# Moving the squares and root of a norm ahead of held-back matrix products in a hybrid encoder layer

## The chip, the cores and the metric

One core of one Trainium2 chip runs the whole layer. The metric is the device time of one execution in microseconds (us); the time before is the median of three executions. Besides these there is one profiled execution, on which every number of the trace rests. The engines are named as in the profile: PE is the matrix engine (PEld its weight loads), DVE the vector engine, ACT the scalar engine, POOL the general-purpose engine, SP the engine that issues most transfers.

## The reference

A layer has a mixer and a gated feed-forward network (FFN), each between two RMS norms:

```python
h = x + rmsnorm(mixer(rmsnorm(x, g_mix_pre)), g_mix_post)
y = h + rmsnorm(conv_ffn(rmsnorm(h, g_ffn_pre)), g_ffn_post)

def conv_ffn(h):
    gate, up = split(h @ w_up)                   # 1024 -> 2 x 2816
    gate_c = causal_dwconv(gate)                 # width 3
    return (gelu(gate_c) * up) @ w_down          # 2816 -> 1024
```

The mixer has one input projection, eight heads of stick-breaking attention, a state-space part with eight heads, and one output projection. There are 2048 prompt rows and 32 sample rows, 1024 features each, in float32. The root of a norm, `rsqrt(mean(h*h) + eps)`, is one number per row.

## The kernel before

Features lie on the partitions and rows (tokens) along the free axis. Every large product is made of three matmuls of rounded halves (hi by hi, hi by lo, lo by hi), recorded in `dense` (L124).

**Stages.** The rows are worked in four blocks `s` = 0 to 3 of 512, 512, 512 and 544 rows. After the input projection of all blocks and the attention of block 0, `build` runs a loop over the blocks: the tail of block `s` (output projection, residual, FFN) is a Python generator, `Tail.stream`, and is fed step by step as filler into the attention of block `s + 1`. A step is one group of three matmuls. For block 3 no attention is left, and its tail runs alone. In the texts "stage s" is the stretch in which the tail of block `s` runs.

**The tail of a stage** (`stream`): eight steps owed by the stage before; `out_units` for half a of the rows (0 to 256 or 272), eight units; `out_units` for half b, with the residual of half a advanced by one feature group every fourth step; the residual of half b; `split` for both halves; the rest of what is owed, 24 steps of the previous block's last down products, held back from its own stage; `root` for both halves; then 22 FFN units `up`, with `down` in groups, and `finish` of the previous block advanced at every second step from unit 1 on.

**What each of these does.** A unit of `out_units` leaves one of eight feature groups in `m[c]` (ACT copy, L915) and adds its square to `msq`. `residual` takes the post-norm's root from `msq`, then for each of the eight groups loads `x` into `xr` (two buffers), scales `m[c]` (DVE, L931), adds `x` (POOL and DVE in turn, L935) and stores it. `split` makes hi (ACT, L948) and lo (DVE, L949) of `m[c]` times the FFN gain. `root` squares and sums the eight `m[c]` again, now for the FFN's input norm, and takes the root with `rstd_narrow`. `up` multiplies the gate product by that root `r` as it leaves PSUM (L984), so the matmuls of `up` need `split` alone.

**Shared buffers.** `square` (L754) writes its square straight into the sum for the first group (L758); for the other seven ACT squares into `sqt` (L761), of which there is one buffer, and POOL adds (L762). All sums of squares use this one `sqt`: those of `out_units` (`msq`), of `root` (`msq` again), of the down products (`fsq`, L1058) and of the attention (`sq`). `rstd_steps` takes two tiles of the PSUM tile `u`, of which there is one buffer: for the column sums (L166), and for the root broadcast again over partitions (L195), which ACT copies out (L201). In stages 0 to 2 the second product of each FFN unit, `up`'s L1006 to L1013, is written to the same `u`; the gate products go to `o`, which has two buffers. In stage 3 the FFN products go to `t` and `o`.

**Order.** The program states an order; a list scheduler that works with simulated times then sets the order of each engine's queue when the kernel is built, and may put an instruction ahead of an earlier one that isn't ready. `pin` and `mark` keep the filler's matmuls behind the attention's matmuls issued ahead of them. On the chip each queue runs in its fixed order.

Of the kernel before, what the change touches and what calls it, by code (L numbers as in the profile page):

```python
# [57 lines left out]
def tiles_of(n):  # L58
    return [(0, n)] if n <= 512 else [(0, n // 2), (n // 2, n)]
# [810 lines left out]
class Tail:  # L870
# [48 lines left out]
    def residual(self, s, half):  # L919

        kn, nc, att = self.kn, self.kn.nc, self.att
        t0 = SBS[s][0]
        c0, c1 = half
        n = c1 - c0
        rm = att.tmp.tile([P, 272], F32, name="rstd")
        kn.rstd_narrow(att.tmp, *kn.bank, [self.msq[:, c0:c1]], n, D, out=rm)
        yield
        for c, m in enumerate(self.m):
            x = (self.late or att.tmp).tile([P, 272], F32, name="xr", bufs=8 if self.late else 2)
            nc.sync.dma_start(x[:, :n], kn.a["xT"][:, c, t0 + c0 : t0 + c1])  # L930
            nc.vector.scalar_tensor_tensor(  # L931
                m[:, c0:c1], m[:, c0:c1], kn.col(C_GMIXP + c), rm[:, :n], op0=ALU.mult, op1=ALU.mult
            )
            eng = nc.vector if c % 2 else nc.gpsimd
            eng.tensor_tensor(m[:, c0:c1], m[:, c0:c1], x[:, :n], op=ALU.add)  # L935
            nc.sync.dma_start(kn.hS[s][:, c, c0:c1], m[:, c0:c1])
            yield

    def split(self, s, half):
# [14 lines left out]
    def root(self, s, half):  # L954
        kn, nc, att = self.kn, self.kn.nc, self.att
        c0, c1 = half
        if c0 == 0:
            self.r = self.rp.tile([P, 544], F32, name="r", bufs=1)
        for c, m in enumerate(self.m):
            att.square(self.msq[:, c0:c1], m[:, c0:c1], c == 0)  # L960
        col = self.rp.tile([P, 8], F32, name=f"rcol{int(c0 > 0)}")
        kn.rstd_narrow(att.tmp, *kn.bank, [self.msq[:, c0:c1]], c1 - c0, D, out=self.r[:, c0:c1], rcol=col)
        self.cols[s, c0] = col
# [116 lines left out]
    def stream(self, s, cat):  # L1080
        nt = SBS[s][1]
        a, b = (0, nt // 2), (nt // 2, nt)
        owed, self.owed = self.owed or iter(()), None
        yield from islice(owed, 8)
        yield from self.out_units(s, cat, a)
        chain = self.residual(s, a)
        for n, _ in enumerate(self.out_units(s, cat, b)):
            yield
            if n % 4 == 0:
                next(chain, None)  # L1090
        for _ in self.residual(s, b):
            pass
        self.split(s, a)
        self.split(s, b)
        yield from owed
        self.root(s, a)
        self.root(s, b)
        done = iter(())
        if s:
            done = (i for h in (0, SBS[s - 1][1] // 2) for i in self.finish(s - 1, h, h + 256, self.f))  # L1100
        groups = self.GROUPS
        tiles = tiles_of(nt)
        acts = {}
        for g, (j0, n) in enumerate(groups):
            acts[g] = []
            for j in range(j0, j0 + n):
                for i, _ in enumerate(self.up(s, j, acts[g])):
                    yield
                    if j and i % 2:
                        next(done, None)  # L1110
                if j == j0 and g and g < len(groups) - 1:
                    yield from self.down(s, g - 1, acts.pop(g - 1), tiles)
        g = len(groups) - 1

        def last():
            for t in [tiles] if s < NSB - 1 else [[t] for t in tiles]:
                for e in range(2):
                    yield from self.down(s, g - 1 + e, acts[g - 1 + e], t, e == 1)
                if s == NSB - 1:
                    for _ in self.finish(s, *t[0], self.f):  # L1120
                        pass

        self.owed = last()
# [167 lines left out]
```

## Time and profile before

| | us |
|---|---|
| median of three executions | 3099.98 (3099.88 to 3104.38) |
| the profiled execution, its own time | 3103.09 |
| its span, first to last instruction | 3101.2 |
| PE busy in the span | 2883.8 |
| DVE, POOL, ACT busy | 1690.6, 1364.9, 1236.7 |
| POOL, sums of squares into `msq` (L762) | 112 instructions of 721 to 1707 ns |
| mean granted PE clock | 0.965 of full speed |

In rows of a timeline the columns are the start, the duration, the engine and line, the operation, its tiles (out<-in), how many instructions are merged, and in brackets the idle time before it with what ended it. In rows of stretches (windows) they are the stretch, its length, each engine's busy time with its count of instructions, the granted clock of PE, the share of DMA and GB/s. In rows of one line they are the count, the shortest, median and longest duration in ns, and when the first and the last began.

### The profile page before, as it was taken

Reading aid. Unit: us, or ns where it says so; the run is one execution under the profiler, and the core shown is the slowest. Engines: PE = TensorE matmul, PEld = TensorE weight load, DVE = VectorE, ACT = ScalarE, POOL = GpSimd, SP = SyncE. Lnnn points to the kernel's source line nnn. Section 1 sums busy time; section 2 is a strip of 40 time slices with the busy share of each in tenths; the row PEclk is TensorE's granted clock in tenths of the full one; section 3 lists DMA queues with packets and bytes.
Section 4 is the critical chain, followed back from the end, with each engine's and each line's share of the span. In section 5 each row is a group of like instructions: output and inputs, shape, how many; then the busy total and the mean of one; then the engine's idle time right before and its main releaser. Section 6 shows DMA issues by size and latency. Waiting matters only on the chain.

```text
span 3101.2 us, 43193 instructions
## 1 busy us (share of the span) xinstructions
PE 2883.8 (93%) x16175; PEld 2345.9 (76%) x16175; DVE 1690.6 (55%) x2388; ACT 1236.7 (40%) x2504; POOL 1364.9 (44%) x1073
## 2 busy tenths in 40 slices
PE   8999999987879999998899999988999999899996
PEld 6777778865747787785577788855777779799996
DVE  6667667656685643439844443398444324523334
ACT  4344444355565443346633322466433213321111
POOL 4555454355777665547732221376322214511113
PEclk9999999999889999998899999999999999899998
DMA  4545454565655778875264455742645554555455
GB/s 169 175 144 175 138 170 116 165 206 179 234 186 190 246 262 274 277 253 177 89 207 166 165 193 180 251 144 82 211 159 174 201 194 154 175 193 177 165 187 168
DMA packets 234658, 571.57 MB, mean 184 GB/s; under 512 B 49514, under 2 KB 101362, under 8 KB 205906
## 3 DMA queue, kind: packets, MB, share of 16 engines
q1 hardware_dynamic: 234450, 568.81, 55.3%
q8 instruction: 129, 2.11, 0.3%
q14 instruction: 79, 0.65, 0.1%
HBM read 435.22 MB, written 133.50 MB: 183 GB/s over the span
## 4 chain that ended last, share of the span: by engine, by line
PE 62%; DVE 17%; DMA 6%; POOL 6%; ACT 4%; issue 4%; SPq 1%; DVEq 0%; POOLq 0%; ACTq 0%
PE o L124 32%; PE u L124 10%; PE t L124 9%; DVE prow L659 4%; PE pa L837 3%; PE pt L822 2%; POOL beta L664 2%; PE z L801 2%; PE o L365 2%; DVE xc L341 1%; DVE acB L436 1%; POOL msq L762 1%; DMA acB<-acD 1%; DVE f L1072 1%; DVE xc L337 1%
## 5 line engine op out<-in xcount | busy, mean ns | idle before, releaser
L124 PE MATMUL o<-xhi,w 128*128 128x512 f32 (+2 forms) x3968 | 1037.5, 346 | 38.3 <-DMA w<-wS_out 8.8
L124 PEld LDWEIGHTS o<-xhi,w 128*128 128x128 f32 x3968 | 698.2, 192 | 138.8 <-issue 16.9
L124 PE MATMUL o<-xlo,w 128*128 128x512 f32 (+2 forms) x1984 | 684.9, 345 | 9.0 <-DVE xlo L273 4.2
L109 POOL TENSOR_TENSOR w<-wraw,w 128x1024 fp32r<-128x1024 f32 (+2 forms) x156 | 377.0, 2417 | 252.6 <-ACT w L108 237.9
L664 POOL TENSOR_TENSOR beta<-beta,prow 128x512 f32<-128x512 f32 (+3 forms) x264 | 313.5, 1192 | 335.0 <-DVE prow L659 317.5
L124 PEld LDWEIGHTS o<-xlo,w 128*128 128x128 f32 x1984 | 381.0, 192 | 55.5 <-DVE xlo L273 6.0
L1005 POOL TENSOR_TENSOR y<-y,gb 128x512 f32<-128x512 f32 (+1 forms) x88 | 118.3, 1344 | 597.9 <-ACT gb L1004 589.1
L659 DVE TENSOR_TENSOR_SCAN prow<-gam,prow 128x513 f32<-128x513 f32 x200 | 321.0, 1610 | 82.8 <-ACT gam L656 75.2
L124 PE MATMUL u<-xhi,w 128*128 128x512 f32 x1056 | 347.6, 400 | 2.2 <-DVE y L1014 2.1
L124 PE MATMUL o<-ah,w 128*128 128x512 f32 x992 | 334.5, 403 | 9.0 <-DVE f L1051 8.8
L124 PEld LDWEIGHTS u<-xhi,w 128*128 128x128 f32 x1056 | 200.4, 190 | 54.6 <-issue 4.2
L822 PE MATMUL pt<-ident,beta 128*128 128x128 f32 x1088 | 186.4, 293 | 51.8 <-POOL beta L664 37.9
L822 PEld LDWEIGHTS pt<-ident,beta 128*128 128x128 f32 x1088 | 133.7, 148 | 131.3 <-POOL beta L664 61.5
L124 PEld LDWEIGHTS o<-ah,w 128*128 128x128 f32 x992 | 187.7, 189 | 58.6 <-DVE f L1051 11.1
L124 PE MATMUL u<-xlo,w 128*128 128x512 f32 x528 | 210.7, 399 | 0.0
L997 DVE SCALAR_TENSOR_TENSOR y<-gb,cv,y 128x512 f32<-128x512 f32 (+1 forms) x176 | 159.9, 909 | 81.1 <-ACT y L995 78.2
L108 ACT CAST w<-wraw 128x1024 fp32r<-128x1024 f32 (+2 forms) x156 | 155.2, 995 | 118.6 <-PE o L124 49.6
L825 ACT COPY wt<-pt 128x512 f32<-128x512 f32 (+3 forms) x282 | 146.4, 532 | 130.9 <-PE pt L822 127.6
L659 DVE TENSOR_TENSOR_SCAN prow<-gam,ones 128x129 f32<-128x129 f32 (+4 forms) x130 | 142.9, 1109 | 101.9 <-ACT gam L656 101.5
L652 ACT ACTIVATE beta<-z 128x512 f32<-128x512 f32 (+2 forms) x330 | 180.4, 547 | 45.2 <-PE z L801 27.5
L124 PE MATMUL o<-al,w 128*128 128x512 f32 x496 | 197.2, 398 | 0.0
L124 PE MATMUL t<-xhi,w 128*128 128x272 f32 x960 | 190.5, 294 | 4.5 <-DMA w<-wS_up 3.3
(255 smaller groups left out, 4999.0 us busy)
## 6 DMA issues: line engine op xcount, KB each, us to landing
w<-wS_up SPq DMA_DIRECT2D x132, 1024.0 KB, 4.8
w<-wS_dn SPq DMA_DIRECT2D x72, 768.0 KB, 4.8
wS_up<-w SPq DMA_DIRECT2D x44, 1024.0 KB, 4.8
w<-wS_out SPq DMA_DIRECT2D x39, 1024.0 KB, 6.2
wraw<-wup SPq DMA_DIRECT2D x44, 512.0 KB, 5.9
k<-kS SPq DMA_DIRECT2D x80, 256.0 KB, 3.7
wS_dn<-w SPq DMA_DIRECT2D x24, 768.0 KB, 4.5
w<-wS_dn SPq DMA_DIRECT2D x32, 512.0 KB, 4.4
```

The costliest lines, as they stand in the source:

```text
L108: nc.scalar.copy(hi[:, :n, :], raw[:, :n, :])
L109: nc.gpsimd.tensor_tensor(lo[:, :n, :], raw[:, :n, :], hi[:, :n, :].bitcast(F32), op=ALU.subtract)
L124: mm = nc.tensor.matmul(ps[:, : c1 - c0], l[:, k, :], at(r, k0 + k)[:, c0:c1], start=first and i == 0 and k == 0, stop=last and i == 2 and ...
L365: nc.tensor.matmul(vp[h][:q, :260], l[k][:, b * P : b * P + q], rr[:, k, h * 260 : h * 260 + 260], start=i == 0 and k == 0, stop=i == 2 an ...
L652: nc.scalar.activation(b[:, :n], z, AF.Sigmoid, scale=0.125)
L659: nc.vector.tensor_tensor_scan(back(pr), back(g), back(g), self.kn.ones[:, 0:1] if prev is None else prev, op0=ALU.mult, op1=ALU.bypass,)
L664: eng.tensor_tensor(b[:, :n], b[:, :n], pr[:, c0 + 1 : 513], op=ALU.mult)
L822: mm = nc.tensor.transpose(t[:, P * j : P * j + P], w[:, P * j : P * j + P], kn.ident[:])
L825: copy(wt[:, : n // P, P * b : P * b + P], t[:, :n].rearrange("p (i q) -> p i q", q=P))
L837: nc.tensor.matmul(av[DH * (j % 2) : DH * (j % 2) + DH, c0:], v[:, j, :], wt[:, j, c0:], start=kc == s and j < 2, stop=kc == 0 and j > 1,)
L997: nc.vector.scalar_tensor_tensor(y[:, :W], gb[:, i : i + W], kn.col(wc + i), y[:, :W], op0=ALU.mult, op1=ALU.add)
L1005: nc.gpsimd.tensor_tensor(y[:, :W], y[:, :W], t, op=ALU.mult)
```

## The change

The squares of the FFN input's norm move out of `root` into `residual`, right behind the sum and the store of each `m[c]`. The root of half a is taken ahead of the residual of half b, and the root of half b behind the two splits, ahead of the owed products. No instruction is added or taken away; the number and sizes of all operations stay the same.

```diff
@@ residual
             eng.tensor_tensor(m[:, c0:c1], m[:, c0:c1], x[:, :n], op=ALU.add)
             nc.sync.dma_start(kn.hS[s][:, c, c0:c1], m[:, c0:c1])
+            att.square(self.msq[:, c0:c1], m[:, c0:c1], c == 0)
             yield
@@ root
             self.r = self.rp.tile([P, 544], F32, name="r", bufs=1)
-        for c, m in enumerate(self.m):
-            att.square(self.msq[:, c0:c1], m[:, c0:c1], c == 0)
         col = self.rp.tile([P, 8], F32, name=f"rcol{int(c0 > 0)}")
@@ stream
                 next(chain, None)
+        self.root(s, a)
         for _ in self.residual(s, b):
             pass
         self.split(s, a)
         self.split(s, b)
+        self.root(s, b)
         yield from owed
-        self.root(s, a)
-        self.root(s, b)
         done = iter(())
```

## The prediction

> **What bounds the kernel now.** I read the page first, then the busy time of each engine by stretch, then the timelines of PE, ACT and POOL around the four roots.
>
> ```profile
> PE 2883.8 (93%) x16175; PEld 2345.9 (76%) x16175; DVE 1690.6 (55%) x2388; ACT 1236.7 (40%) x2504; POOL 1364.9 (44%) x1073
> ```
>
> PE is the bound on average, but an average over stages says little of one step. The stretches say more (all engines, then the transposes L822 alone; the last row is a piece of the chain of waits, 24 packed matmuls in 5.60 us):
>
> ```profile
> 909.00:938.00 29.00, 22.32 (x117) 13.39 (x114) 24.59 (x22) 19.88 (x50) 24.60 (x23) 0.88 0.43 139
> 1340.00:1380.00 40.00, 40.00 (x312) 36.21 (x311) 8.50 (x14) 14.55 (x36) 14.27 (x19) 1.00 0.68 237
> 1443.00:1517.00 74.00, 60.69 (x283) 34.67 (x282) 60.23 (x51) 53.96 (x126) 62.38 (x53) 0.82 0.25 80
> 2054.00:2136.00 82.00, 64.06 (x314) 35.47 (x313) 68.12 (x53) 60.09 (x137) 66.05 (x57) 0.88 0.24 71
> 2250.00:2350.00 100.00, 100.00 (x456) 76.20 (x455) 46.59 (x56) 33.83 (x70) 23.99 (x22) 1.00 0.48 167
> ```
>
> ```profile
> 909.00:938.00 29.00, 8.09 (x44) 5.38 (x44) 0.88 0.43 139
> 1443.00:1517.00 74.00, 22.24 (x121) 15.25 (x120) 0.82 0.25 80
> 2054.00:2136.00 82.00, 23.93 (x135) 15.87 (x134) 0.88 0.24 71
> 2250.00:2350.00 100.00, 8.73 (x53) 6.46 (x53) 1.00 0.48 167
> ```
>
> ```profile
> 2250.00:2350.00 100.00, 82.53 (x345) 64.01 (x344) 1.00 0.48 167
> ```
>
> ```profile
> 1100.32 5.60 PE o L124 x24
> ```
>
> From 2250 to 2350 PE is packed: 345 filler matmuls (the row of L124) at 5.60/24 = 0.233 us take 80.5 us, and the other 19.5 us carry 53 transposes, four to an attention slot, so 13.25 slots at 1.47 us of PE each. In the first, third and fourth stretch above the filler stands still and only attention runs: 44, 121 and 135 transposes are 11, 30 and 34 slots, worth 16, 44.5 and 50 us of packed PE in 29, 74 and 82 us. So 0.44, 0.40 and 0.395 of these stretches is **lost PE time**: the rest would have to be done anyway. Since PE is packed later in each stage, time won here passes to the end.
>
> Why does the filler stand? Stage 1, PE and ACT:
>
> ```profile
> 1371.57 0.42 ACT L758 ACTIVATE msq<-m 128x256 f32<-128x256 f32 x1
> 1459.62 0.44 ACT L761 ACTIVATE sqt<-m 128x256 f32<-128x256 f32 x1
> 1516.64 0.40 ACT L201 COPY r<-u 128x256 f32<-128x256 f32 x1
> ```
>
> ```profile
> 1442.82 0.39 PE L124 MATMUL o<-xhi,w 128*128 128x512 f32 x1
> 1517.41 0.40 PE L124 MATMUL u<-xhi,w 128*128 128x512 f32 x1
> 1531.54 0.50 PE L166 MATMUL u<-ones,fsq 128*128 128x1 f32 x4
> 1542.75 0.48 PE L124 MATMUL u<-xhi,w 128*128 128x512 f32 x1
> ```
>
> The gate product of FFN unit 0 is done at 1443; its second product needs `u`, and gets it at 1517.4, straight after the copy of the second root. The first square of root a, which needs no `sqt`, ran as early as 1371.6. The next, which needs `sqt`, waits until 1459.6, behind the whole `fsq` chain. So `sqt` is handed out in program order, and so is `u`. The chains themselves:
>
> ```profile
> L762 POOL TENSOR_TENSOR msq<-msq,sqt x14: 727/736/1114, 1341.3 to 1397.3; 128x256 f32<-128x256 f32 x14
> L762 POOL TENSOR_TENSOR fsq<-fsq,sqt x14: 725/914/1642, 1416.9 to 1457.0; 128x256 f32<-128x256 f32 x14
> L762 POOL TENSOR_TENSOR msq<-msq,sqt x14: 721/1550/1661, 1460.2 to 1508.8; 128x256 f32<-128x256 f32 x14
> L762 POOL TENSOR_TENSOR msq<-msq,sqt x14: 722/1416/1657, 2074.7 to 2129.0; 128x256 f32<-128x256 f32 x14
> L762 POOL TENSOR_TENSOR fsq<-fsq,sqt x9: 732/738/895, 2641.3 to 2651.7; 128x256 f32<-128x256 f32 x9
> ```
>
> A square and its add take, from start to start, (1457.0 - 1416.9)/13 = 3.1 us for `fsq`, 3.7 and 4.2 us for the roots of stages 1 and 2, and 10.4/8 = 1.3 us in stage 3, where no attention competes.
>
> **The change, part by part.** *Removed and added:* nothing. 64 squares, 56 adds and eight roots change place; no DMA moves, and SP's queue keeps its order.
>
> *Squares and root of half a* go into the output projection of half b. The second stretch above (1340 to 1380) has PE full, with ACT busy for 14.55 and POOL for 14.27 us of 40; seven pairs there cost 7 x (0.42 + 0.74) = 8 us on the two engines, and are hidden by PE. Lost cover would cost those 8 us per stage, more at the slower pace (rival 3).
>
> But they stand in the `sqt` order ahead of the projection's last four squares of half b, and those start the residual of half b. Rows of the last sum of half a (DVE L935), and of the last such square and the last sums of half b:
>
> ```profile
> 1392.02 0.90 DVE L935 TENSOR_TENSOR m<-m,xr 128x256 f32<-128x256 f32 x1
> 2008.30 0.95 DVE L935 TENSOR_TENSOR m<-m,xr 128x256 f32<-128x256 f32 x1
> 2049.01 0.90 DVE L935 TENSOR_TENSOR m<-m,xr 128x256 f32<-128x256 f32 x1
> 900.67 1.15 DVE L935 TENSOR_TENSOR m<-m,xr 128x256 f32<-128x256 f32 x1 [0.48 <-DMA xr<-xT]
> ```
>
> ```profile
> 2008.12 0.84 POOL L762 TENSOR_TENSOR msq<-msq,sqt 128x256 f32<-128x256 f32 x1 [0.82 <-ACT sqt L761]
> ```
>
> ```profile
> L935 DVE TENSOR_TENSOR m<-m,xr x4: 393/524/886, 1420.0 to 1435.9; 128x256 f32<-128x256 f32 x4
> ```
>
> Stage 1: the sum ends at 1392.9; then five pairs (the last of a, four of b), at 2.5 us between 1.3 and 3.7, end at 1405.4, against 1398.4 before (last add at 1397.3): the residual of half b starts **7 us later**. Stage 2: 2009.3 + 12.5 = 2021.8 against 2009.0, 13 us later. For stage 0 I take 6 us. Root a (one `u` pass, about 7 us) fits beside these pairs.
>
> *Squares and root of half b* now follow each sum. Stage 1: the last sum ends at 1436.3, moved to 1443, its square at 1446. The root takes from the last add (1508.8 + 1.6) to the first use of `u` (1517.4) 7 us, so `u` is free at 1453: unit 0 runs on almost without a stop.
>
> *What is late next:* `fsq`. Its 14 pairs now start behind root b at 1446, not at 1417. `finish` takes `u` ahead of unit 1's second product, which before came 11.2 us after the first `fsq` column sum (1531.54 to 1542.75). With 3.1 us a pair: 1446 + 43 + 11 = 1500, against 1542.75. Stage 1 gains 42 us of standing, x 0.40 = **17 us**.
>
> Stage 2, and stage 0, where nothing is owed and no `finish` runs:
>
> ```profile
> 2158.54 0.39 PE L124 MATMUL u<-xhi,w 128*128 128x512 f32 x1
> ```
>
> ```profile
> 938.18 0.40 PE L124 MATMUL u<-xhi,w 128*128 128x512 f32 x1
> ```
>
> Stage 2: 2049.9 + 13 + 3 + 43 + 11 = 2120 against 2158.5: 38 x 0.395 = **15 us**. Stage 0: 901.8 + 6 + 3 + 7 = 918 against 938.2: 20 x 0.44 = **9 us**.
>
> Stage 3 runs alone, and PE waits for the squares and the root openly:
>
> ```profile
> 2661.57 1.15 PE L166 MATMUL u<-ones,msq 128*128 128x1 f32 x6 [5.19 <-POOL msq L762]
> 2663.96 1.46 PE L195 MATMUL u<-ident,rcol 128*128 128x128 f32 x6 [1.24 <-POOL rcol L184]
> 2666.37 0.59 PE L124 MATMUL t<-xhi,w 128*128 128x272 f32 x1 [0.95 <-DVE gb L984]
> ```
>
> 5.19 + 1.24 + 0.95 = 7.4, and some slow matmuls behind it: **8 us**, between 0 (if `finish` fills the gap) and 13.
>
> Sum: 9 + 17 + 15 + 8 = 49 us. On the profiled execution that is 3103.1 - 49 = 3054; its own time lies 3.1 us over the median, so on the median 3100.0 - 49 = **3051.0**. The bounds come from the pace of an `fsq` pair: at 1.3 us stages 1 and 2 give 27 and 25, the sum 69 (3031); at 4.2 us 11 and 9, the sum 37 (3063). I take 3.1, the pace of the same chain under the same attention.
>
> Two rules of the Trainium skill bear on this. POOL's add has a median of 736 ns where DVE is busy for 8.5 of 40 us, and of 1550 ns where it is busy for 60 of 74. The Trainium skill, "GPSIMD Engine Reference", section 8 (Key points), says that POOL shares its SBUF interfaces with the vector engine and is held up by vector instructions with two SBUF inputs; the trace agrees. It speaks against the change, since half a's adds move beside the residual's two-input sums on DVE and `fsq` moves deeper into the attention; by it alone the sum is the 37 us of the 4.2 us pace. The other is in rival 1.
>
> **The rivals.**
>
> 1. *PE's busy time is real work.* Then only 22, 18 and 22% of the three stretches is idle (22.32 of 29, 60.69 of 74, 64.06 of 82), and the gain is 20 x 0.23 + 42 x 0.18 + 38 x 0.22 + 8 = 28 us: **3072**. Against it stands the count of slots. A new order of the queues, which loses part of the gain, ends here too. The Trainium skill, "Perfetto Trace Analysis", section Identifying the Most-Contended Engine, says that matmul busy time misleads and weight-load time is to be read; PEld has 34.67 of 74 here and 76.20 of 100 when packed, which gives 39% lost, as the slots do.
>
> 2. *No effect.* The scheduler may already place what is ready, as it did with the square at 1371.6; then moving lines changes nothing: **3100**. Against it stands the 88 us between that square and the next one.
>
> 3. *Slower.* ACT works its queue in order. The squares of half a wait in it for POOL's release of `sqt`, and behind them wait the copies (L915) that free `o` for the projection, which now fills PE to 40 of 40 us. The price is the wait per square, for 7 squares in 3 stages. At 49/21 = 2.3 us each all is given back; at the roots' full pace, 4.2 us, it costs 21 x 4.2 - 49 = 39 us: **3139**. For it speaks that the pace has been 3.7 and 4.2 us where attention ran; against it, that the projection runs with the 736 ns adds.
>
> **How the numbers follow.** Forecast 0.58, with its own range 3031 to 3063; rival 1 0.22; rival 2 0.07; rival 3 0.13. Within 0.2% is about what a measurement of this kernel can tell from no change. So faster 0.80, same 0.07, slower 0.13. The range of 8 in 10 takes in the forecast's bounds with 9 us below for stage 3 and the slots, and rival 1 with some 20 us above: 3022 to 3092.
>
> **What would show it.** Right: in stages 1 and 2 squares of half a lie between the projection's, `fsq` adds come behind all `msq` adds, `u` starts within some 10 us of the end of unit 0's gate, and the next stop, before unit 1's second product, ends with the `fsq` root near 1500 and 2120; in stage 3 the 5.19 us wait is gone. Wrong: PE idle in the output projection with ACT as releaser, root matmuls standing in PE's queue for POOL, or a stage that ends no earlier although its stop is shorter.

## The result, and the profile after

The changed kernel takes 3066.39 us (median; 3062.08 to 3073.27) against 3102.18 us of the kernel before, measured beside it: a ratio of **0.9884** with a 95% interval of 0.9859 to 0.9910, 36 us faster. The profiled executions stand at 3063.36 and 3103.09 us, 39.7 us apart; on these the readings rest.

The busy time of the engines, from the page of the changed kernel:

```profile
PE 2862.1 (93%) x16175; PEld 2331.6 (76%) x16175; DVE 1671.4 (55%) x2388; ACT 1236.2 (40%) x2504; POOL 1338.1 (44%) x1073
```

The instructions are the same in number; PE is busy for 21.7 us less, POOL for 26.8 us less. To see where the time went I cut the span into stages at the first square of each output projection (L758, written straight into `msq`). The timeline of ACT, the kernel before:

```profile
797.22 0.41 ACT L758 ACTIVATE msq<-m 128x256 f32<-128x256 f32 x1
1337.48 0.42 ACT L758 ACTIVATE msq<-m 128x256 f32<-128x256 f32 x1
1951.60 0.42 ACT L758 ACTIVATE msq<-m 128x256 f32<-128x256 f32 x1
2577.88 0.44 ACT L758 ACTIVATE msq<-m 128x272 f32<-128x272 f32 x1
```

and the changed kernel:

```profile
798.48 0.42 ACT L758 ACTIVATE msq<-m 128x256 f32<-128x256 f32 x1
1338.15 0.42 ACT L758 ACTIVATE msq<-m 128x256 f32<-128x256 f32 x1
1937.35 0.42 ACT L758 ACTIVATE msq<-m 128x256 f32<-128x256 f32 x1
2541.47 0.43 ACT L758 ACTIVATE msq<-m 128x272 f32<-128x272 f32 x1
```

With the ends of the spans, 3101.2 and 3061.5, these are the lengths:

| stage | before, us | after, us | gain | forecast |
|---|---|---|---|---|
| 0 | 540.3 | 539.7 | 0.6 | 9 |
| 1 | 614.1 | 599.2 | 14.9 | 17 |
| 2 | 626.3 | 604.1 | 22.2 | 15 |
| 3 | 523.3 | 520.0 | 3.3 | 8 |

(The part ahead of stage 0 became 1.3 us longer.) Nearly all of the gain lies in stages 1 and 2. Stages 0 and 1 hold nearly the same work in both kernels, stages 2 and 3 don't: PE does 97 products into `t` ahead of the last of these squares before, and 62 after, and the other 35 fall into stage 3. At 0.126 us each (103 of them take 13 us from 2577 to 2590 in the kernel before) that is some 4 us. So like for like stage 2 gains some 18 us, and stage 3 some 8.

The rows that answer to the prediction's, from the timeline of PE: the first use of `u` by FFN unit 0 of stage 0; the end of unit 0's gate product, the first use of `u` by unit 0, the `fsq` column sum and the first use of `u` by unit 1, all of stage 1; unit 1 of stage 2.

```profile
952.10 0.48 PE L124 MATMUL u<-xhi,w 128*128 128x512 f32 x1
...
1460.28 0.39 PE L124 MATMUL o<-xhi,w 128*128 128x512 f32 x1
...
1473.99 0.39 PE L124 MATMUL u<-xhi,w 128*128 128x512 f32 x1
...
1502.44 0.61 PE L166 MATMUL u<-ones,fsq 128*128 128x1 f32 x4
...
1518.33 0.47 PE L124 MATMUL u<-xhi,w 128*128 128x512 f32 x1
...
2107.74 0.48 PE L124 MATMUL u<-xhi,w 128*128 128x512 f32 x1
```

Stages begin at other times in each kernel, so from here on such a time is counted from its stage's start. Unit 1 of stage 1 gets `u` at 180.2 instead of 205.3 us, and unit 1 of stage 2 at 170.4 instead of 206.9. In stage 0, unit 0 gets it *later*, at 153.6 instead of 141.0.

The stops of the filler did shrink by as much as was forecast. In stage 1 it stood 74.2 us ahead of unit 0's second product and 14.0 ahead of unit 1's; now it stands 13.3 and 33.0, which is 42 us less. But the gate product of unit 0, which needs the residual and the split of both halves, ends 122.5 us after the stage's start instead of 105.7, and these 17 us go off again.

The reason stands on POOL: the power operation (L184) of the post-norm's root of half b, with which the residual of half b begins, in stages 0 to 3. Before:

```profile
872.30 1.36 POOL L184 TENSOR_TENSOR rn_v<-rn_v,mhalf 128x2 f32<-128x2 f32 x1
1406.22 1.63 POOL L184 TENSOR_TENSOR rn_v<-rn_v,mhalf 128x2 f32<-128x2 f32 x1
2016.45 1.63 POOL L184 TENSOR_TENSOR rn_v<-rn_v,mhalf 128x2 f32<-128x2 f32 x1
2625.13 0.86 POOL L184 TENSOR_TENSOR rn_v<-rn_v,mhalf 128x3 f32<-128x3 f32 x1 [4.01 <-DVE rn_v L176]
```

After:

```profile
897.24 1.62 POOL L184 TENSOR_TENSOR rn_v<-rn_v,mhalf 128x2 f32<-128x2 f32 x1
1427.47 0.71 POOL L184 TENSOR_TENSOR rn_v<-rn_v,mhalf 128x2 f32<-128x2 f32 x1
2018.98 1.62 POOL L184 TENSOR_TENSOR rn_v<-rn_v,mhalf 128x2 f32<-128x2 f32 x1
2604.33 0.86 POOL L184 TENSOR_TENSOR rn_v<-rn_v,mhalf 128x3 f32<-128x3 f32 x1 [6.91 <-DVE rn_v L176]
```

Counted from the stage's start it comes 24, 21, 17 and 16 us later than before (872.30 - 797.22 = 75.1 against 897.24 - 798.48 = 98.8, and so on).

In stage 3 the open wait of 5.19 us for the root's squares is gone. In its place the timelines of PE and, in the last row, ACT show:

```profile
2619.55 0.60 PE L124 MATMUL t<-xlo,w 128*128 128x272 f32 x1 [2.51 <-DVE xlo L950]
...
2634.43 0.60 PE L124 MATMUL t<-xhi,w 128*128 128x272 f32 x1 [3.17 <-DMA w<-wS_up]
...
2679.30 0.59 PE L124 MATMUL t<-ah,w 128*128 128x272 f32 x1 [6.35 <-ACT f L1048]
...
2678.87 0.67 ACT L1048 COPY f<-t 128x272 f32<-128x272 f32 x2 [4.39 <-DMA o_yT<-f]
```

The 6.35 us are new: the first down products of stage 3 wait for their copy into `f`, and the copy waits until `finish` of block 2 has stored the old `f`. `fsq` comes behind root b now, so that store is late.

### The profile page after: what moved, and what is told of

It is laid out like the page before. It is cut to its first block, busy times and chain, and to the rows that moved or that the text cites. A ratio compares the mean times of both kernels' runs of the same rounds, so it can differ in the third digit from the quotient of the medians.

```text
span 3061.5 us, 43141 instructions
## 1 busy us (share of the span) xinstructions
PE 2862.1 (93%) x16175; PEld 2331.6 (76%) x16175; DVE 1671.4 (55%) x2388; ACT 1236.2 (40%) x2504; POOL 1338.1 (44%) x1073
## 4 chain that ended last, share of the span: by engine, by line
PE 62%; DVE 16%; DMA 8%; POOL 5%; ACT 4%; issue 3%; SPq 1%; DVEq 0%; POOLq 0%; ACTq 0%
PE o L124 30%; PE t L124 10%; PE u L124 10%; DVE prow L659 3%; PE pa L837 3%; PE pt L822 2%; PE z L801 2%; PE o L365 2%; POOL beta L664 2%; DVE xc L341 2%; DMA wraw<-wup 1%; DVE xlo L950 1%; POOL w L109 1%; DMA xr<-xT 1%; DVE acB L436 1%
## 5 line engine op out<-in xcount | busy, mean ns | idle before, releaser
L124 PEld LDWEIGHTS o<-xhi,w 128*128 128x128 f32 x3968 | 696.7, 192 | 127.3 <-issue 10.2
L664 POOL TENSOR_TENSOR beta<-beta,prow 128x512 f32<-128x512 f32 (+3 forms) x264 | 310.0, 1179 | 433.5 <-DVE prow L659 415.2
L109 POOL TENSOR_TENSOR w<-wraw,w 128x1024 fp32r<-128x1024 f32 (+2 forms) x156 | 368.0, 2359 | 255.8 <-ACT w L108 235.3
L659 DVE TENSOR_TENSOR_SCAN prow<-gam,prow 128x513 f32<-128x513 f32 x200 | 311.4, 1560 | 113.3 <-ACT gam L656 104.8
L996 DVE SCALAR_TENSOR_TENSOR y<-gb,cv,y 128x512 f32<-128x512 f32 (+1 forms) x176 | 166.1, 945 | 88.2 <-ACT y L994 85.4
L822 PEld LDWEIGHTS pt<-ident,beta 128*128 128x128 f32 x1088 | 132.4, 147 | 104.4 <-issue 35.4
L822 PE MATMUL pt<-ident,beta 128*128 128x128 f32 x1088 | 181.0, 289 | 32.8 <-POOL beta L664 15.8
L108 ACT CAST w<-wraw 128x1024 fp32r<-128x1024 f32 (+2 forms) x156 | 155.1, 994 | 114.6 <-DMA wraw<-wup 69.4
```

The source lines that it names most:

```text
L108: nc.scalar.copy(hi[:, :n, :], raw[:, :n, :])
L109: nc.gpsimd.tensor_tensor(lo[:, :n, :], raw[:, :n, :], hi[:, :n, :].bitcast(F32), op=ALU.subtract)
L124: mm = nc.tensor.matmul(ps[:, : c1 - c0], l[:, k, :], at(r, k0 + k)[:, c0:c1], start=first and i == 0 and k == 0, stop=last and i == 2 and ...
L659: nc.vector.tensor_tensor_scan(back(pr), back(g), back(g), self.kn.ones[:, 0:1] if prev is None else prev, op0=ALU.mult, op1=ALU.bypass,)
L664: eng.tensor_tensor(b[:, :n], b[:, :n], pr[:, c0 + 1 : 513], op=ALU.mult)
L822: mm = nc.tensor.transpose(t[:, P * j : P * j + P], w[:, P * j : P * j + P], kn.ident[:])
```

## The experiments

All kernels are timed against the kernel before on the same chip; "before" in a diff is the kernel before, "changed" the changed one. The theories are named in the order in which they came up.

### Theory A: the order in which sqt is handed out

A says that the filler stands because root's squares wait for `sqt` behind the whole `fsq` chain. The first kernel takes that wait away with a buffer of its own and moves no line.

```diff
@@ before, root
-            att.square(self.msq[:, c0:c1], m[:, c0:c1], c == 0)
+            att.square(self.msq[:, c0:c1], m[:, c0:c1], c == 0, "sqr")
```

> The kernel before, with one edit: the squares of root get a buffer of their own in place of the shared sqt. All lines stay at their old place, behind the owed products. Theory A (what holds the filler is the order in which the one sqt is handed out: root's squares behind fsq): nearly all of the gain of the change comes without moving a line, and stage 0 gains too, since no square of the output projection is delayed: 3035 to 3065 us, the filler's stop in stage 1 (before: 1443 to 1517) shorter by 40 us or more. Theory B (the place of root's steps in the program, ahead of the owed products, is what counts): no difference, 3095 to 3105.

Measured: 3028.14 us, ratio 0.9776 (0.9755 to 0.9796). Twice the gain of the change, with no line moved: the sharing of `sqt` is what the kernel before paid for, and B falls. The gain is 7 us beyond A's range.

The second leaves the squares in `root` and moves only the two root calls ahead of the owed products.

```diff
@@ before, stream
-        yield from owed
         self.root(s, a)
         self.root(s, b)
+        yield from owed
```

> The kernel before, with both roots whole (squares inside) put behind the two splits and ahead of the owed products. Stage 0 owes nothing and is the same program as before. Theory A: root's squares come behind the output projection's and ahead of fsq, the residual of half b isn't delayed, so stages 1 and 2 gain as in the change or more (15 to 25 us each), stage 0 nothing: 3050 to 3070. Theory C (the gain of the change is that half a's squares are worked in the output projection): most of it goes, 3080 to 3095.

Measured: 3033.82 us, 0.9785 (0.9767 to 0.9804). C falls, and A's range ends 16 us above it: this order alone, with the squares still in `root`, gives more than the change does. So something in the change costs about 30 us against this simpler order.

The third keeps the change's squares in `residual` and puts both root calls back behind the owed products.

```diff
@@ changed, stream
-        self.root(s, a)
         for _ in self.residual(s, b):
             pass
         self.split(s, a)
         self.split(s, b)
-        self.root(s, b)
         yield from owed
+        self.root(s, a)
+        self.root(s, b)
```

> The changed kernel with both root calls back at their old place behind the owed products; the squares stay in residual. Theory A: sqt is handed out in the same order as in the change, and the residual of half b no longer waits for root a's pass through u: as the change or a little faster, 3055 to 3068. Theory B: the gain goes, 3090 to 3102.

Measured: 3059.80 us, 0.9875 (0.9856 to 0.9894), no slower than the change itself: with the squares in `residual`, the new place of the root calls adds nothing.

The fourth gives the changed kernel the buffer of the first one, so that half a's squares no longer stand ahead of the projection's in `sqt`.

```diff
@@ changed, residual
-            att.square(self.msq[:, c0:c1], m[:, c0:c1], c == 0)
+            att.square(self.msq[:, c0:c1], m[:, c0:c1], c == 0, "sqr")
```

> The changed kernel with a buffer of their own for root's squares. Theory A with its refinement (in the change the output projection's last squares of half b stand behind half a's squares in sqt, which starts the residual of half b some 25 us late in stages 0 and 1): the delay goes, stage 0 gains 10 us and stages 1 and 2 about 10 us more each: 3030 to 3050. If the late start of the residual costs nothing, because owed products fill PE: 3060 to 3070, like the change.

Measured: 3063.35 us, 0.9886 (0.9865 to 0.9907). The refined A missed. In stage 1 (timelines of POOL and PE) root a's power operation, the residual's of half b, root b's, and unit 1's `u` come at

```profile
1415.34 1.63 POOL L184 TENSOR_TENSOR rcol<-rcol,mhalf 128x2 f32<-128x2 f32 x1
...
1425.56 1.36 POOL L184 TENSOR_TENSOR rn_v<-rn_v,mhalf 128x2 f32<-128x2 f32 x1
...
1482.68 1.62 POOL L184 TENSOR_TENSOR rcol<-rcol,mhalf 128x2 f32<-128x2 f32 x1
...
1507.17 0.48 PE L124 MATMUL u<-xhi,w 128*128 128x512 f32 x1
```

The residual's root is as late as in the change (88.3 us after the start at 1337.26), although `sqt` no longer holds it: now it stands behind root a's two `u` tiles, which are handed out in program order too.

### Theory D: two ways to hold back the residual of half b

D says that each of the two ways, `sqt` and `u`, holds back the residual of half b by itself, and that this delay is what the change loses. Four kernels: only the way through `u` (the root calls of the change in the kernel before, squares still in `root`); neither way (the second kernel with an own buffer; and the changed kernel with an own buffer and root a behind the residual of half b); only the way through `sqt` (the last one without the own buffer).

```diff
@@ before, stream (the first kernel)
+        self.root(s, a)
         for _ in self.residual(s, b):
             pass
         self.split(s, a)
         self.split(s, b)
+        self.root(s, b)
         yield from owed
-        self.root(s, a)
-        self.root(s, b)
```

```diff
@@ changed, stream (the last two kernels)
-        self.root(s, a)
         for _ in self.residual(s, b):
             pass
         self.split(s, a)
         self.split(s, b)
+        self.root(s, a)
         self.root(s, b)
         yield from owed
```

> The kernel before with the two root calls at the change's places (half a ahead of the residual of half b, half b behind the splits), the squares still inside root, one sqt. Theory D (the change loses about 30 us because the residual of half b is held back in two ways, each enough by itself: through sqt, since half a's squares stand ahead of the projection's last squares of half b, and through u, since root a's two u tiles stand ahead of the residual's two): here only the way through u is left. The residual's root of half b comes some 15 to 25 us later than before, and the time is 3050 to 3075. Rival E (the order of u costs nothing; what the second kernel of this study gained, 3034, stays): 3028 to 3042, with that root within 5 us of before.

Measured: 3084.84 us, 0.9955 (0.9939 to 0.9971). The residual's root of stage 1 comes at 98.7 us, 30 later than before. The sign is D's, the size is beyond its range; E falls.

> The kernel before with both roots whole ahead of the owed products and with an own buffer for their squares. If the two gains are of different waits (the wait of unit 0 for root behind fsq, and the wait of unit 1 for fsq behind root) they add up in part: 3012 to 3024. If both edits lift the same wait and nothing else, it ends where the better of the two did: 3025 to 3036.

Measured: 3030.48 us, 0.9771 (0.9750 to 0.9791): the two edits lift the same wait.

> The changed kernel with an own buffer for the squares of root, and with root a moved behind the residual of half b (both roots behind the splits, ahead of the owed products). Theory D: both ways that hold the residual of half b are gone, its root comes within 5 us of before, and the time is 3020 to 3038. Rival F (the squares inside the residual cost by themselves, by POOL and ACT beside the residual's sums): the time stays at 3052 to 3068 although that root comes in time.

Measured: 3024.34 us, 0.9754 (0.9734 to 0.9773). F falls: the squares cost nothing where they stand in `residual`. The residual's root of stage 1 comes at 78.3 us, 10 later than before rather than within 5. The first kernel, which moves no line, has it at 77.7, so these 10 us come with the own buffer; why is open.

> The changed kernel with root a moved behind the residual of half b, one sqt as in the change. Theory D: the way through sqt is left and is enough by itself, so the residual's root of half b still comes some 10 to 25 us later than before and the time is 3048 to 3068. If the order of u was the only cause: 3025 to 3040.

Measured: 3059.68 us, 0.9878 (0.9858 to 0.9898), with that root at 87.8 us. Either way is enough to hold it back, and both must be opened.

### Theory H: the end of the chain

D still took the delay itself for the price, and the order for the only cause. Two kernels with a second shared `sqt` tested that, in the kernel before and in the changed one.

```diff
@@ square
-            t = self.tmp.tile([P, 272], F32, name="sqt")[:, : sq.shape[-1]]
+            t = self.tmp.tile([P, 272], F32, name="sqt", bufs=2)[:, : sq.shape[-1]]
```

> The kernel before with two buffers of sqt instead of one, shared as before; no line moved. Theory D says that what costs the time is the order in which sqt is handed out (root's squares behind the whole fsq chain), not the number of buffers: with two in rotation the root's squares still stand behind all fsq squares but the last, only the pace of a pair may fall somewhat. So the second root of stage 1 still comes late (its power operation over 160 us after the stage's start, where the kernel with an own buffer had it at 125 and the kernel before at 174) and the time is 3070 to 3098. Rival G (any further buffer does it, the chains were slow because a square and its add could not overlap): 3025 to 3050.

Measured: 3052.89 us, 0.9855 (0.9832 to 0.9877), with the second root of stage 1 at 142.6 us. D missed, and G by 3 us: the pace of the pairs counts for far more than D allowed.

> The changed kernel with two shared buffers of sqt. Theory D: the order through sqt and through u stays, so the residual's root of half b still comes 10 us or more later than before in stages 0 and 1, and the time is 3045 to 3066. Rival G: 3022 to 3040, with that root within 5 us of before.

Measured: 3026.82 us, 0.9774 (0.9753 to 0.9795). **D falls** as a statement on the price. The residual's root of half b is still late, by 20 us in stage 0 and 13 in stage 1, and yet the span is 35 us below the change's (3026.7 against 3061.5). G's time came in, but not its sign, that this root comes within 5 us of before. The timelines of POOL and PE (the residual's root in stages 0 and 1, unit 1's `u`), with stages that start at 798.25 and 1336.90:

```profile
893.54 1.62 POOL L184 TENSOR_TENSOR rn_v<-rn_v,mhalf 128x2 f32<-128x2 f32 x1
...
1418.75 0.70 POOL L184 TENSOR_TENSOR rn_v<-rn_v,mhalf 128x2 f32<-128x2 f32 x1
...
1489.40 0.48 PE L124 MATMUL u<-xhi,w 128*128 128x512 f32 x1
```

Unit 1 gets `u` at 152.5 us, against 180.2 in the change. The groups of L762 in stage 1 show the pace; first the changed kernel, then the one with two buffers:

```profile
L762 POOL TENSOR_TENSOR fsq<-fsq,sqt x14: 722/736/1641, 1469.8 to 1504.7; 128x256 f32<-128x256 f32 x14
```

```profile
L762 POOL TENSOR_TENSOR fsq<-fsq,sqt x14: 720/1173/1657, 1454.5 to 1476.5; 128x256 f32<-128x256 f32 x14
```

The pairs come every (1504.7 - 1469.8)/13 = 2.7 us with one buffer and every 1.7 us with two, although the median add is longer with two (1173 against 736 ns). So the work in a pair doesn't set the pace. Some of the changed kernel's pairs, from the timeline of POOL:

```profile
1475.61 0.74 POOL L762 TENSOR_TENSOR fsq<-fsq,sqt 128x256 f32<-128x256 f32 x1
1476.30 3.99 POOL L664 TENSOR_TENSOR beta<-beta,prow 128x512 f32<-128x512 f32 x2
1480.26 1.19 POOL L762 TENSOR_TENSOR fsq<-fsq,sqt 128x256 f32<-128x256 f32 x1
1481.97 0.73 POOL L762 TENSOR_TENSOR fsq<-fsq,sqt 128x256 f32<-128x256 f32 x1 [0.53 <-ACT sqt L761]
1483.23 0.74 POOL L762 TENSOR_TENSOR fsq<-fsq,sqt 128x256 f32<-128x256 f32 x1 [0.53 <-ACT sqt L761]
```

With nothing between two adds a round trip between ACT and POOL through the one buffer takes 1.26 us (1481.97 to 1483.23). The slow pairs have attention's products (L664, 2.0 us each) between their adds. With one buffer an add can't follow the last one until ACT has squared again, and other work of the queues stands in between; with two, some adds come back to back (1468.56, 1469.71 and 1470.86 in that kernel).

So theory H: what counts is when `u` reaches units 0 and 1, at the end of the chain residual of half b, root b, `fsq`. A delay at its head and the pace of its pairs are terms of one sum. Two kernels were forecast from it: the second and the ninth (root a late) with two buffers.

> The kernel before with both roots whole ahead of the owed products, and two shared buffers of sqt: two lines of edit. Theory H (what counts is when u reaches units 0 and 1 of a stage, at the end of the chain residual of half b, root b, fsq; a delay at its head and the pace of its pairs are terms of the same sum, and in stage 2 nothing is left to win below some 170 us): the residual's root of half b in stage 1 stays within 5 us of before (68.7 us after the stage's start), unit 1 gets u at 135 to 152 us instead of 159, and the time is 3010 to 3030. If the pace were of no account beside that residual: 3030 to 3038, as with one buffer.

Measured: **3011.45 us, 0.9707 (0.9689 to 0.9726)**, the fastest of all: two edits, one moved line and one more buffer. In stage 1, from 1327.28: the residual's root at 71.6 us, root b's, and `u` for units 0 and 1, the last at 138.1.

```profile
1398.87 0.71 POOL L184 TENSOR_TENSOR rn_v<-rn_v,mhalf 128x2 f32<-128x2 f32 x1
...
1441.92 0.70 POOL L184 TENSOR_TENSOR rcol<-rcol,mhalf 128x2 f32<-128x2 f32 x1
...
1447.11 0.47 PE L124 MATMUL u<-xhi,w 128*128 128x512 f32 x1
...
1465.38 0.39 PE L124 MATMUL u<-xhi,w 128*128 128x512 f32 x1
```

> The changed kernel with root a moved behind the residual of half b, and two shared buffers of sqt. Theory H: unit 1 of stage 1 gets u at 140 to 155 us instead of 178, although the residual's root of half b still comes over 5 us later than before, and the time is 3015 to 3032. If the delay of that residual had a price of its own, whatever the end of the chain: 3040 to 3060, as with one buffer.

Measured: 3026.20 us, 0.9755 (0.9735 to 0.9774); the residual's root at 80.9 us, unit 1 at 156.7 (2 us past H's range). Both times lie in H's ranges.

The grid of order and buffers, as ratios to the kernel before:

| order | one `sqt` | two shared | own one for root |
|---|---|---|---|
| before | 1 | 0.9855 | 0.9776 |
| roots whole, ahead of owed | 0.9785 | **0.9707** | 0.9771 |
| the change | 0.9884 | 0.9774 | 0.9886 |
| the change, root a late | 0.9878 | 0.9755 | 0.9754 |

And stage 1 of all profiled executions, in us from its start (the times of the rows that were shown, read in the same way in each trace):

| kernel | span | residual b's root | root b | unit 1's `u` | stage length |
|---|---|---|---|---|---|
| before | 3101.2 | 68.7 | 174.3 | 205.3 | 614.1 |
| root calls of the change only | 3082.5 | 98.7 | 145.1 | 194.4 | 607.4 |
| changed | 3061.5 | 89.3 | 130.6 | 180.2 | 599.2 |
| squares of the change only | 3063.0 | 88.0 | 130.6 | 175.0 | 602.2 |
| changed, root a late | 3056.7 | 87.8 | 131.9 | 177.7 | 602.9 |
| changed, own buffer | 3057.6 | 88.3 | 145.4 | 169.9 | 603.5 |
| before, two `sqt` | 3055.8 | 69.1 | 142.6 | 167.1 | 603.0 |
| roots ahead | 3041.3 | 69.4 | 112.8 | 159.1 | 587.1 |
| changed, root a late, two `sqt` | 3028.1 | 80.9 | 121.8 | 156.7 | 589.1 |
| changed, two `sqt` | 3026.7 | 81.8 | 120.6 | 152.5 | 582.2 |
| changed, own buffer, root a late | 3022.5 | 78.3 | 126.2 | 150.2 | 582.4 |
| roots ahead, own buffer | 3020.3 | 78.1 | 125.2 | 150.0 | 581.6 |
| before, own buffer | 3023.9 | 77.7 | 124.7 | 148.2 | 581.2 |
| roots ahead, two `sqt` | 3008.6 | 71.6 | 114.6 | 138.1 | 574.4 |

A profiled execution can lie some 9 us from the median of its kernel (with the roots ahead 3043.1 against 3033.8), so small differences between rows mean little.

Over these fourteen the span follows unit 1's `u` with a correlation of 0.99, root b with one of 0.85, and the residual's root with one of 0.28. A straight line gives 0.61 us of stage 1 for each us that unit 1 gets `u` earlier, but that is not the price of the standing, since part of it is attention that changes stage. The transposes of attention (L822) in stage 1 are 352 in the first seven kernels of the table and 319 to 344 in the other seven, which have as many more in stage 2. The two kernels farthest from the line (the changed one with an own buffer, and the one before with two `sqt`, 8 and 9 us above it) are the two of the first seven with the earliest `u`.

Stages 1 and 2 taken together are nearly free of this. From the kernel before to the fastest they shorten from 1240.4 to 1176.7 us, and the two times of unit 1's `u` add up to 276.4 instead of 412.2 us. A straight line over all fourteen gives 0.44 us for each us of that sum. By the same count the clause of H that stage 2 has nothing left to win below 170 us isn't borne out: its length stays between 599 and 611 us there, but it takes up to 33 transposes more.

## Why the prediction was right, and where it was not

The direction and the cause held: 36 us of gain against 49. So did the wide range, 3022 to 3092; the forecast's own, 3031 to 3063, was missed by 3 us. The sum hides several errors.

- **The lost PE time** was counted as 0.40 of the standing in stages 1 and 2 (and 0.44 in stage 0). Unit 1 got `u` earlier by 205.3 - 180.2 = 25.1 us in stage 1 and by 206.9 - 170.4 = 36.5 in stage 2, and the stages gained 14.9 and, like for like, some 18 us: 0.59 and 0.50. Over all fourteen kernels, stages 1 and 2 together, it was 0.44, so 0.40 was nearly right in general and too low for this change. In stage 1 one can see where the difference lies. These are the transposes of attention (L822) ahead of unit 1's `u` and behind it, before and after (the stretch, its length, PE and PEld with their counts, the clock, the DMA share, GB/s):

```profile
1337.48:1542.75 205.27, 37.23 (x210) 26.49 (x210) 0.91 0.50 164
1542.75:1951.60 408.85, 22.55 (x142) 17.49 (x142) 0.99 0.53 184
1338.15:1518.33 180.18, 27.29 (x168) 19.86 (x168) 0.95 0.53 178
1518.33:1937.35 419.02, 27.84 (x184) 22.20 (x184) 1.00 0.53 183
```

  The 42 transposes, or 10.5 attention slots, that no longer run ahead of `u` cost 419.02 - 408.85 = 10.2 us behind it, 0.97 us a slot, where the prediction had 1.47. Some 4 us of that can be the granted clock of the later stretch, 1.00 against 0.99 (an estimate, 0.01 x 409); the rest is open. How much of the factor is the lower clock of the standing itself, 0.91 and 0.95 ahead of `u`, no run separates. Rival 1, which took PE's busy time as work, put the factor at 0.18 and 0.22 (its 22% for the first stretch is 23%, as its sum has it), too low by every count. Its 3072 lies nearer to the result than 3051 by luck, because the saved standing was overrated in both. The weight-load rule of the Trainium skill ("Perfetto Trace Analysis", Identifying the Most-Contended Engine) gave 39%, near the 0.44 over all kernels and below the 0.59 and 0.50 of this change.
- **The delay of the residual of half b** is the step that failed. It was put at 6, 7 and 13 us from the `sqt` order, and root a was to "fit beside". It was 24, 21 and 17 us. The way through `sqt` alone makes 19 us of it in stage 1 (87.8 against 68.7), and so does the way through `u` (88.3, and 98.7 with the squares still in `root`), which the prediction didn't price, though it had found that `u` is handed out in program order.
- **Stage 1**: unit 0 got `u` at 1474 instead of 1453, so the `fsq` chain began later; its pace was 2.7 instead of 3.1 us, but from the column sum to unit 1 went 15.9 us (1502.44 to 1518.33) instead of 11. Saved standing of 25 instead of 42 us, times a factor of 0.59 instead of 0.40, makes 15 against 17: two errors that cancelled, by luck.
- **Stage 2**: unit 1 was forecast at 2120, which is 168.4 us from the old start, and came at 170.4. The standing was right. Like for like it gave some 18 us against 15, which is the factor; the other 4 of the 22 are products that now fall into stage 3.
- **Stage 0** was to give 9 and gave 0.6. Unit 0 got `u` not 20 us earlier but 13 later. With the chain really shortened the stage does pay: in the fastest kernel `u` comes at 126.0 and the stage takes 529.6 us, 10.7 less. Why 13 us later cost nothing isn't settled.
- **Stage 3** was to give 8 and gave 3.3, or some 8 without the 35 products that it took over from stage 2. The wait of 5.19 went, so that the sum came out right by luck: what the prediction had as the way to zero (that `finish` fills the gap) was not it, but a wait for `finish`: 6.35 us for the old `f`, and 2.51 for `xlo` of a late half b.

That squares of half a would cost little in the output projection was right. The first stretches of PE in stage 1 in the changed kernel (the stretch, its length, PE's busy time with its count, the clock, the DMA share, GB/s):

```profile
1338.15:1358.15 20.00, 20.00 (x157) 1.00 0.75 277
1358.15:1378.15 20.00, 20.00 (x166) 1.00 0.58 208
1378.15:1398.15 20.00, 18.50 (x117) 1.00 0.79 260
```

Nearly all of the squares of half a fall into the third stretch. PE idles there for 1.50 us, against 0.44 in the same stretch before, and that wait is one of an owed product for DVE (L1050), not for ACT. The projection's last copy (L915) begins 55.2 us after the stage's start, against 57.2 before. So rival 3 (ACT's queue holds up the projection) didn't come. The rule on POOL and DVE ("GPSIMD Engine Reference", section 8 of the Trainium skill), which would have made the `fsq` pairs slow, didn't decide: their adds had a median of 736 ns, less than the 914 before. Rival 2 is out by the interval.

## What to carry to other kernels

A tile with one buffer that several chains share is a queue in program order: before an edit moves one user ahead, list who stands behind it in *each* such tile (here `sqt` and `u`), and price the first one that is needed soon. Follow the chain to its last user and score an edit by when that one starts, not by the stop that it removes. Where a chain alternates between two engines through one buffer, try a second buffer as well: here it took 0.8 to 1.5% off in each of four orders, and the best kernel has it together with the simplest reordering.

## What was not expected

The pace of a square and its add is set by the hand-over, and by what stands between two of them in the queues, not by the work of the pair: 0.42 us on ACT and 0.74 us on POOL took 2.7 us a pair with one buffer, and 1.7 us with two, while the add itself grew to 1.17 us. A length of a stage is a price only for the same work: by stage 1 alone the standing seemed to cost 0.61 us per us, by stages 1 and 2 together 0.44. And the changed kernel does the same instructions with 26.8 us less of busy time on POOL and 19.2 us less on DVE (1690.6 to 1671.4): busy times of these engines are no fixed price that can be carried from one order to another.
